# Sharing one load of the first FFN's gate and up weights between the first two row tiles

## The chip, the cores and the metric

The kernel runs on the 8 cores of one Trainium2 chip. Each core computes one of eight batch entries, so the cores do equal work and exchange nothing. The metric is device time in microseconds (us) of the slowest core.

Some executions fall into a slower state in which one die (cores 0 to 3, or 4 to 7) or both get a lower TensorE clock, whatever the kernel. The profile of the kernel before fell into the slow state on die 0; I read it on core 4, which lies on the undisturbed die, and I read core 4 of every other kernel too unless the text says otherwise. Where the cores of one run differ, I give the range or the mean of all eight (of cores 4 to 7 for the kernel before).

Engine names in the profile: PE is TensorE (matmuls), DVE is VectorE, ACT is ScalarE, POOL is GpSimd, SP issues DMA.

## The reference, cut to what matters

```python
D_MODEL, BATCH, SEQ, D_FF = 1024, 8, 4096, 2816
# x = x + 1/2 * SwiGLU_1(RMSNorm(x))
# h = RMSNorm(x);  [q,k,v | u,v_s | gates] = h @ W_in
# y_att = chunked attention (9-chunk band, relative bias);  y_sgu = spatial gating on 128-frame blocks
# x = x + (sigmoid(g_att) * (y_att @ W_att) + sigmoid(g_sgu) * (y_sgu @ W_sgu)) @ W_out
# x = x + 1/2 * SwiGLU_2(RMSNorm(x));  out = RMSNorm_final(x)
def rmsnorm(x, g):
    xf = x.astype(jnp.float32)
    y = xf * lax.rsqrt(jnp.mean(xf * xf, axis=-1, keepdims=True) + EPS)
    return (y * g.astype(jnp.float32)).astype(x.dtype)

def swiglu(h, w_gate, w_up, w_down):
    return (jax.nn.silu(h @ w_gate) * (h @ w_up)) @ w_down
```

Weights are fp32 in memory, and matmuls run in bf16. A core has 4096 rows, cut into 8 tiles of 512 rows. The factor `rsqrt(mean(x²))` is one number per row, so it can be applied before the gate and up matmuls or to their results. The change uses that.

## The kernel before: the parts that matter

Weights stream through a ring in SBUF in chunks: one gate/up chunk is 2 MB of fp32 in memory and 1 MB of bf16 in the ring. The first use of a chunk is a GpSimd DMA that casts. At one of its first uses, chosen by a rule, the bf16 chunk is also written back to a scratch in memory; from then on SP loads that half-sized copy.

```python
# pump(): as soon as the ring has room, issue the next chunk's load
if chunk not in converted:
    ...
    p.dma("pool", lambda e, dst=dst, src=src: e.dma_start(out=dst, in_=src), writes=res, sem=f"slotq{i}")
    if u >= (first_seen[chunk] * 2) % NREP:      # the rule: at which use it is written back
        converted.add(chunk); pending_wb[k] = (chunk, scr, dst, i)
else:
    p.dma("sp", ...)                             # load the bf16 copy

def dense_bank():                                # four PSUM banks in turn for all dense matmuls
    b = dn[0] % 4; dn[0] += 1; return b

def tg_buf():                                    # six work buffers in turn, for every engine
    i = tg[0] % 6; tg[0] += 1; return TG[i], ("TG", i)
```

A tile's RMSNorm is `nsq` (squares on ScalarE, summed on GpSimd or VectorE), `nstat` (a matmul with ones gives the row sums; ScalarE makes the factor), and `napply` (VectorE writes normalized bf16 to `XT`). Side work is hung on numbered pieces of the TensorE program ("hooks"). Attention of a tile is a generator that is interleaved with the next tile's FFN; at the end of each head pair it copies from PSUM, takes reciprocals on VectorE, multiplies, and lets GpSimd check the range:

```python
# attention: end of a head pair
yu, yres = tg_buf(); r2, rres = tg_buf()
... four copies PSUM -> r2, yu (VectorE and ScalarE) ...
def recip(i, j): ... e.reciprocal(out=r2[:, sl], in_=r2[:, sl])                   # VectorE, twice
def weigh(i):
    ... e.tensor_tensor(out=YA[:, hp, :], in0=yu[:], in1=r2[:], op=ALU.mult)      # VectorE
    for val, op in ((R_LO, ALU.is_ge), (R_HI, ALU.is_le)):
        buf, bres = tg_buf()
        ... gpsimd tensor_scalar(out=ok, in0=r2, ...); gpsimd tensor_tensor(OKA += ok)

# the program
load_x(0); pump()                                # x of tile 0 and all ring slots at once
for d in range(8): nsq(0, d, "dve")
nstat()
for d in range(8): napply(0, 0, d)
run_all(ffn(0, 0, False, ffn1_hooks(0)))         # FFN 1 of tile 0, whole
nxt_ffn = ffn(1, 0, True, ffn1_hooks(1))
for _ in range(4): next(nxt_ffn)
win(0, {})                                       # input projection of tile 0
for t in range(n_tiles):
    ...
    interleave(main, attention(t), n_main - 6, n_att(t))   # main: FFN 1 of tile t+1
    ...                                          # merge(t), win(t+1), FFN 2 of tile t
```

Of the kernel before, what the change touches and what calls it, by code (L numbers as in the profile page):

```python
# [17 lines left out]
T = 512  # L18
# [3 lines left out]
NREP = 3  # L22
# [21 lines left out]
class Prog:  # L44
# [58 lines left out]
    def dma(self, queue, fn, reads=(), writes=(), sem=None):  # L103
        op = _Op(queue, fn, is_dma=True, semkey=("dma", sem))
        op.idx = len(self.ops[queue])
        self._track(op, reads, writes)
        c = self.dma_counts.get(sem, 0) + 16
        self.dma_counts[sem] = c
        op.count = c
        self.ops[queue].append(op)  # L110
        return op
# [58 lines left out]
def interleave(main, side, n_main, n_side):  # L170
    done = 0
    for i in range(n_main):
        next(main, None)
        want = (i + 1) * n_side // n_main
        while done < want:
            next(side, None)
            done += 1
    for _ in side:
        pass


def build_nc(n_tiles=NT):
# [28 lines left out]
    with ExitStack() as st:  # L211
# [52 lines left out]
        EBS = X[2][:].rearrange("p a b -> p (a b)")[:, 0:8 * 384].rearrange("p (h u) -> p h u", h=8)  # L264
# [8 lines left out]
        def run(p, dry):  # L273
# [29 lines left out]
            def pump():  # L303
                while nxt[0] < len(chunk_order) and (general[0] or nxt[0] < fast_len[0]):
# [19 lines left out]
                    if chunk not in converted:  # L324
                        u = uses.get(chunk, 0)
                        uses[chunk] = u + 1
                        if chunk not in first_seen:
                            first_seen[chunk] = len(first_seen)
                        p.dma("pool", lambda e, dst=dst, src=src: e.dma_start(out=dst, in_=src),
                              writes=res, sem=f"slotq{i}")  # L330
                        if u >= (first_seen[chunk] * 2) % NREP:
# [6 lines left out]
            def get_slot(chunk):  # L338
# [7 lines left out]
                if k in pending_wb:  # L346
                    chunk_, scr, dst, i = pending_wb.pop(k)
                    p.dma("sp", lambda e: e.dma_start(out=scr, in_=dst),
                          reads=res, writes=[("SCR", chunk_)], sem=f"wb{i}")
# [7 lines left out]
            def load_x(t):  # L357
                b = t % 3
                step = 1 if t == 0 else 4
                for d in range(0, 8, step):  # L360
# [3 lines left out]
                          writes=[("X", b, i) for i in range(d, d + step)], sem=f"x{b}{d}")  # L364

            dn = [0]

            def dense_bank():
                b = dn[0] % 4
# [10 lines left out]
            def const_loads():  # L380
                p.dma("sp", lambda e: e.dma_start(out=BG[:], in_=bgate_d), writes=["BG"], sem="c2")
# [4 lines left out]
                p.dma("sp", lambda e: e.dma_start(out=EBS, in_=ebsrc_d), writes=[("X", 2, i) for i in range(8)], sem="c3")  # L386
                p.dma("pool", lambda e: e.dma_start(out=WST[:], in_=wst_d), writes=["WST"], sem="c8")
                p.dma("pool", lambda e: e.dma_start(out=IDB[:], in_=ident_d), writes=["IDB"], sem="c7")

            def const_ops():  # L390
# [13 lines left out]
                p.dma("sp", lambda e: e.dma_start(out=rt, in_=relt_d[:, 0:512]), writes=[bres], sem="c9")  # L404
# [19 lines left out]
            def bias_exp(i):  # L424
                h0 = 2 * i
                p.add("act", lambda e: e.activation(out=EB[:, h0:h0 + 2, 0:384], in_=EBS[:, h0:h0 + 2, :], func=AF.Exp),
                      reads=[("X", 2, j) for j in range(8)], writes=[("EB", i)])
# [24 lines left out]
            def nstat():  # L452
# [4 lines left out]
                p.add("act", lambda e: e.activation(out=RSTD[:], in_=bank(b), func=AF.Ln, bias=EPSB[:]),  # L457
                      reads=[rb(b), "EPSB"], writes=["RSTD"])
                p.add("act", lambda e: e.activation(out=RSTD[:], in_=RSTD[:], func=AF.Exp, scale=-0.5),  # L459
                      reads=["RSTD"], writes=["RSTD"])  # L460
# [8 lines left out]

            def store(t, d):  # L470
# [6 lines left out]
            def ffn(t, i, use_tanh, hooks=None):  # L477
                hooks = hooks or {}
                xt, xp, b3 = XT[t % 2], t % 2, t % 3
                piece = 0  # L480

                def hook():
                    nonlocal piece
                    if piece in hooks:
                        hooks[piece]()
                    piece += 1

                for f2 in (3, 8, 9, 10, 2, 0, 1, 4, 5, 6, 7):
                    Wc, wres, k = get_slot(("ffs", i, f2))
                    for a in range(2):  # L490
                        fc = 2 * f2 + a
                        W = Wc[:, a * 2048:(a + 1) * 2048]
                        bg, bu = dense_bank(), dense_bank()
                        for kc in range(8):
                            p.add("pe", lambda e, kc=kc, W=W, bg=bg: e.matmul(  # L495
                                bank(bg), lhsT=W[:, kc * 128:(kc + 1) * 128], rhs=xt[:, kc, :], start=(kc == 0), stop=(kc == 7)),
                                reads=wres + [("XT", xp, kc)], writes=[rb(bg)])
                        buf, bres = tg_buf()
                        if use_tanh:
                            p.add("act", lambda e, buf=buf, bg=bg: e.activation(out=buf[:], in_=bank(bg), func=AF.Tanh, scale=0.5),  # L500
                                  reads=[rb(bg)], writes=[bres])
                            p.add("dve", lambda e, buf=buf, bg=bg: e.scalar_tensor_tensor(  # L502
                                out=buf[:], in0=buf[:], scalar=1.0, in1=bank(bg), op0=ALU.add, op1=ALU.mult),
# [606 lines left out]
```

## Time and profile before

| | before |
|---|---|
| fast runs beside the changed kernel | 2813.39, 2810.54, 2814.45 us |
| span of core 4, granted clock | 2806.4 us, 0.994 |
| TensorE busy on core 4 | 2701.7 us, 96% |
| start of the merge of tile 0, core 4 | 335.1 us |
| from one merge to the next, tiles 1 to 6 | 342.2 (343.4 once) |
| from the merge of tile 6 to that of tile 7 | 218.1 us |

"Start of the merge" is the first matmul that reads `YA`, the attention's result.

The cores' spans and clocks of the kernel before:

```profile
core 0: 2974.2 us, clock 0.932
...
core 4: 2806.4 us, clock 0.994
```

The timeline of TensorE at the start of the kernel before (columns: start, duration, engine, line, operation, output and input tiles, shape, count; in brackets the idle time before it and what ended it):

```profile
24.05 0.77 PE L455 MATMUL ps<-ACCR,ONESR 128*128 128x512 f32 x1 [24.05 <-DVE ACCR L447]
27.33 5.22 PE L495 MATMUL ps<-XT,RING 128*128 128x512 bf16 x8 [2.52 <-DVE XT L466]
...
124.87 1.89 PE L511 MATMUL ps<-XT,RING 128*128 128x512 bf16 x7
126.60 3.62 PE L528 MATMUL ps<-HT,RING 128*128 128x512 bf16 x16
```

The first gate matmul starts at 27.3 us, and the 352 gate and up matmuls of tile 0 end at 126.6 us. At one matmul per 0.216 us they are 76.0 us of work, so 50.6 us are lost. The list of waits of TensorE (total, times, longest) shows the largest pieces:

```profile
PE ps L455 <- DVE ACCR L447: 36.0, 11, 24.0
PE ps L687 <- ACT E L691: 10.8, 7, 1.7
PE ps L495 <- DMA RING<-fsrc: 6.8, 4, 3.9
...
PE ps L701 <- DVE TG L711: 5.2, 8, 0.7
```

L455 is the row-sum matmul (24.0 us of its 36.0 at the start), L687 the attention's scores, L701 its second product. Later tiles wait 3.5 us each: they are nearly pure TensorE work.

### The profile page before, as it was taken

How to read it: one execution, taken by the hardware profiler on the slowest of the kernel's cores; microseconds unless marked ns; L12 is line 12 of the kernel's file. 1: busy time of each engine (PE TensorE's matmuls, PEld its weight loads, DVE VectorE, ACT ScalarE, POOL GpSimd, SP SyncE). 2: the span in 40 equal slices, each digit the busy share in tenths (PEclk: the TensorE clock that was granted, in tenths of full speed). 3: DMA queues.
4: the chain of work that ended last, by engine and by line, in shares of the span. 5: the costliest groups of instructions: out<-in, count | busy, mean ns of one | idle time of the engine just before them, and what ended most of it. 6: DMA issues, size and time to landing. Idle time of an engine off the chain costs nothing.

```text
span 2974.2 us, 38345 instructions; the slowest of 8 cores (2802.6 to 2974.2 us)
## 1 busy us (share of the span) xinstructions
PE 2891.8 (97%) x13034; PEld 1288.2 (43%) x13034; DVE 1248.1 (42%) x1929; ACT 893.9 (30%) x1347; POOL 503.3 (17%) x490
## 2 busy tenths in 40 slices
PE   6899999999999999999999999999999999999997
PEld 2344444444444444444444444444444444444443
DVE  2326343263432644336433464324544255455432
ACT  2323232232322323224232232323323233343221
POOL 0212312112111121111211121111211112102111
PEclk9899889998999999999999999999999999999998
DMA  9988999877777554664344443444334443433352
GB/s 194 189 166 209 176 182 176 176 208 175 176 185 184 169 144 154 176 202 170 133 142 144 161 149 135 149 144 164 139 137 140 144 148 133 141 128 123 128 182 78
DMA packets 112517, 472.41 MB, mean 159 GB/s; under 512 B 9144, under 2 KB 9144, under 8 KB 104128
## 3 DMA queue, kind: packets, MB, share of 16 engines
q1 hardware_dynamic: 90288, 371.71, 36.4%
q0 software_dynamic: 21312, 97.10, 20.6%
q8 instruction: 112, 1.84, 0.2%
q10 hardware_dynamic: 720, 1.07, 0.2%
q14 instruction: 85, 0.70, 0.1%
HBM read 501.92 MB, written 65.01 MB: 191 GB/s over the span
## 4 chain that ended last, share of the span: by engine, by line
PE 92%; DMA 3%; DVE 2%; ACT 1%; issue 1%; POOL 0%; DVEq 0%; ACTq 0%; SPq 0%; POOLq 0%
PE ps L528 22%; PE ps L511 20%; PE ps L495 20%; PE ps L810 8%; PE ps L557 6%; PE ps L820 4%; PE ps L570 3%; PE ps L839 3%; PE ps L701 2%; PE ps L687 2%; DMA ffs<-RING 1%; DMA RING<-fsrc 1%; DMA wos<-RING 0%; PE ps L644 0%; PE ps L455 0%
## 5 line engine op out<-in xcount | busy, mean ns | idle before, releaser
L495 PE MATMUL ps<-XT,RING 128*128 128x512 bf16 x2816 | 706.7, 396 | 6.8 <-DVE XT L466 2.5
L511 PE MATMUL ps<-XT,RING 128*128 128x512 bf16 x2816 | 706.8, 397 | 6.3 <-DVE HT L515 6.3
L528 PE MATMUL ps<-HT,RING 128*128 128x512 bf16 x2816 | 660.7, 399 | 0.0
L528 PEld LDWEIGHTS ps<-HT,RING 128*128 128x128 bf16 x2816 | 285.2, 102 | 362.7 <-issue 145.2
L515 DVE TENSOR_TENSOR HT<-ps,TG 128x512 bf16<-128x512 f32 x352 | 241.1, 685 | 466.8 <-PE ps L511 419.0
L511 PEld LDWEIGHTS ps<-XT,RING 128*128 128x128 bf16 x2816 | 281.4, 101 | 351.3 <-issue 121.2
L495 PEld LDWEIGHTS ps<-XT,RING 128*128 128x128 bf16 x2816 | 281.8, 101 | 350.5 <-issue 119.6
L444 POOL TENSOR_TENSOR ACC<-ACC,TG 128x512 f32<-128x512 f32 x186 | 239.8, 1289 | 1075.4 <-ACT TG L441 1074.3
L441 ACT ACTIVATE TG<-X 128x512 f32<-128x512 f32 x224 | 140.2, 627 | 547.5 <-DVE X L534 453.4
L534 DVE SCALAR_TENSOR_TENSOR X<-ps,X 128x512 f32<-128x512 f32 x128 | 88.4, 692 | 424.7 <-PE ps L528 420.8
L810 PE MATMUL ps<-XT,RING 128*128 128x512 bf16 x1024 | 261.1, 401 | 0.0
L506 ACT ACTIVATE TG<-ps 128x512 f32<-128x512 f32 x176 | 105.0, 597 | 449.0 <-PE ps L495 435.4
L691 ACT ACTIVATE E<-ps 128x1024 bf16<-128x1024 f32 (+1 forms) x240 | 168.4, 702 | 197.3 <-PE ps L687 174.3
L732 POOL TENSOR_SCALAR TG<-TG 128x512 bf16<-128x512 f32 x64 | 98.8, 1543 | 587.3 <-DVE TG L721 577.6
L502 DVE SCALAR_TENSOR_TENSOR TG<-TG,ps 128x512 f32<-128x512 f32 x176 | 119.7, 680 | 168.5 <-ACT TG L500 145.3
L500 ACT ACTIVATE TG<-ps 128x512 f32<-128x512 f32 x176 | 105.1, 597 | 266.6 <-PE ps L495 236.1
L557 PE MATMUL ps<-XT,RING 128*128 128x512 bf16 x768 | 178.2, 395 | 0.0
L694 DVE TENSOR_TENSOR E<-E,EB 128x1024 bf16<-128x1024 bf16 (+1 forms) x240 | 127.5, 531 | 94.9 <-ACT E L691 93.9
L824 DVE SCALAR_TENSOR_TENSOR TG<-TG,ps 128x512 f32<-128x512 f32 x128 | 87.8, 687 | 182.1 <-PE ps L820 155.3
L810 PEld LDWEIGHTS ps<-XT,RING 128*128 128x128 bf16 x1024 | 103.8, 102 | 135.1 <-issue 60.2
L815 ACT ACTIVATE TG<-ps,BG 128x512 f32<-128x512 f32 x128 | 87.5, 687 | 241.1 <-PE ps L810 241.0
L466 DVE SCALAR_TENSOR_TENSOR XT<-X,G,RSTD 128x512 bf16<-128x512 f32 x192 | 135.6, 746 | 30.9 <-ACT RSTD L459 30.9
(91 smaller groups left out, 1937.5 us busy)
## 6 DMA issues: line engine op xcount, KB each, us to landing
RING<-ffs SPq DMA_DIRECT2D x131, 1024.0 KB, 5.0
RING<-wds SPq DMA_DIRECT2D x97, 704.0 KB, 4.4
RING<-fsrc POOLq DMA_DIRECT2D x45, 1024.0 KB, 13.4
RING<-mgs SPq DMA_DIRECT2D x48, 768.0 KB, 4.3
RING<-wis SPq DMA_DIRECT2D x29, 1024.0 KB, 4.8
ffs<-RING SPq DMA_DIRECT2D x22, 1024.0 KB, 12.2
RING<-wd POOLq DMA_DIRECT2D x31, 704.0 KB, 11.2
out<-X SPq DMA_DIRECT2D x32, 512.0 KB, 4.1
```

The lines of the kernel that those rows point to most:

```text
L441: p.add("act", lambda e: e.activation(out=buf[:], in_=src, func=AF.Square, scale=1.0 / 32.0), reads=[xres], writes=[bres])
L444: p.add(eng, lambda e: e.tensor_tensor(out=ACC[:], in0=ACC[:], in1=buf[:], op=ALU.add), reads=["ACC", bres], writes=["ACC"])
L466: p.add("dve", lambda e: e.scalar_tensor_tensor(out=dst, in0=src, scalar=G4[:, which * 8 + d:which * 8 + d + 1], in1=RSTD[:], op0=ALU.mult ...
L495: p.add("pe", lambda e, kc=kc, W=W, bg=bg: e.matmul(bank(bg), lhsT=W[:, kc * 128:(kc + 1) * 128], rhs=xt[:, kc, :], start=(kc == 0), stop= ...
L502: p.add("dve", lambda e, buf=buf, bg=bg: e.scalar_tensor_tensor(out=buf[:], in0=buf[:], scalar=1.0, in1=bank(bg), op0=ALU.add, op1=ALU.mul ...
L511: p.add("pe", lambda e, kc=kc, W=W, bu=bu: e.matmul(bank(bu), lhsT=W[:, 1024 + kc * 128:1024 + (kc + 1) * 128], rhs=xt[:, kc, :], start=(k ...
L515: p.add("dve", lambda e, buf=buf, bu=bu, fc=fc: e.tensor_tensor(out=HT[:, fc, :], in0=bank(bu), in1=buf[:], op=ALU.mult), reads=[rb(bu), b ...
L528: p.add("pe", lambda e, fc=fc, W=W, by=by: e.matmul(bank(by), lhsT=W[:, fc * 128:(fc + 1) * 128], rhs=HT[:, fc, :], start=(fc == 0), stop= ...
L557: p.add("pe", lambda e, kc=kc, W=W, b=b, cc=cc: e.matmul(bank(b), lhsT=W[:, kc * 512 + cc * 128:kc * 512 + (cc + 1) * 128], rhs=XT[t % 2][ ...
L691: p.add("act", lambda e: e.activation(out=ee, in_=PS[2][:].rearrange("p (h c) -> p h c", h=2)[:, :, 0:n], func=AF.Exp), reads=[rb(4), rb(5 ...
L694: p.add("dve", lambda e: e.tensor_tensor(out=ee, in0=ee, in1=EB[:, 2 * hp:2 * hp + 2, u0:u0 + n], op=ALU.mult), reads=[("E", i % 2), ("EB" ...
L810: p.add("pe", lambda e, kc=kc, W=W, bgt=bgt, j=j: e.matmul(bank(bgt), lhsT=W[:, j * 1024 + kc * 128:j * 1024 + (kc + 1) * 128], rhs=XT[t % ...
```

## The change

The intent is to lose less at the start. Only x of tile 0 and one chunk (in four parts) load first. TensorE begins on x that is converted but not normalized ("raw"), and tile 0's row factor is applied where results leave PSUM. The gate/up chunks then serve tiles 0 and 1 together, tile 1 four chunks behind, so each fp32 chunk feeds twice the matmuls. Transfers not needed yet are "paced": they wait for the newest TensorE instruction in program order. The down projections and the attention follow:

- before: gate/up/down(0), input projection(0), then gate/up/down(1) interleaved with attention(0), 56 pieces of the FFN;
- after: gate/up(0 and 1), down(0), last chunk of (1), input projection(0), then down(1), 16 pieces, interleaved with attention(0).

The core of the diff:

```diff
+        if paced:
+            op.deps.append(self.ops["pe"][-1])        # a DMA waits for PE's newest instruction
 ...
-                        if u >= (first_seen[chunk] * 2) % NREP:
+                        if k == 0:                    # first chunk in four parts
+                            for j in range(4): ...
+                        else:                         # the second waits for the last part of x of tile 0
+                            ... reads=[("X", 0, 7)] if k == 1 else () ...
+                        if u >= (0 if first_seen[chunk] < 19 else first_seen[chunk] % 2 + 1):
 ...
+            n_dense = [4]                             # 6 banks during the joint stage
 ...
+            def gu_chunk(t, f2, slot, mode, hook, ht=ht_own, free=True):
+                banks = [dense_bank() for _ in range(4)]        # four banks at once (before: two)
+                ...                                             # modes tanh, silu, and for tile 0:
+                        VectorE: buf = bank(bg) * RS0           # raw: row factor on the gate result
+                        ScalarE: buf = Silu(buf)
+                        VectorE: buf = buf * RS0                # and for the up result
+                if mode == "raw_first":                         # first chunk, follows x piece by piece
+                    for kc in range(8):
+                        nraw(t, 0, kc)
+                        for j in range(4): mm(j, kc)
+                        ...
+            def gate_up_both(hooks):
+                LAG = 5
+                for n in range(len(F2) + LAG - 1):
+                    if n >= LAG:
+                        f2 = F2[n - LAG + 1]
+                        writeback(slots[f2])
+                        yield from gu_chunk(1, f2, slots[f2], "silu", hook, ht_second)
+                    if n < len(F2):
+                        f2 = F2[n]
+                        slots[f2] = get_slot(("ffs", 0, f2), wb=(n == 0))
+                        n_dense[0] = 6
+                        yield from gu_chunk(0, f2, slots[f2], "raw" if n else "raw_first", hook, free=(n == 0))
 ...
+                add_hook(hk, 4, P(load_x, 1))                   # x of tile 1, paced
 ...
-            run_all(ffn(0, 0, False, ffn1_hooks(0)))
-            nxt_ffn = ffn(1, 0, True, ffn1_hooks(1))
+            run_all(gate_up_both(both_hooks()))
+            run_all(down(0, 0, 0.5, Hooks(hk)))
+            run_all(gu_chunk(1, F2[0], get_slot(("ffs", 0, F2[0])), "silu", Hooks(hk), ht_second))
             win(0, {})
 ...
+                    if t == 0:
+                        main = down(1, 0, 0.5, Hooks(hk), ht_second)
+                        interleave(main, attention(t), 14, n_att(t))
+                    else:                                       # attention starts 6 pieces later than before
+                        main = ffn(t + 1, 0, True, ffn1_hooks(t + 1))
+                        interleave(main, attention(t), N_FFN - 6, n_att(t), 6)
```

## The prediction

> **What bounds it now.** The fast runs take 2810.5 and 2813.4 us; the profile fell in the slow state, so I read core 4 of the fast die (2806.4 us, clock 0.994). TensorE is the limit: its busy row is 9 in 38 of 40 slices, matmuls start every 0.216 us, and the chain of waits is 89% TensorE. Only the start is loose. By the timeline the first gate matmul starts at 27.3 us, and the gate/up of tile 0 (352 matmuls, 76 us of pure work) ends at 126.6: 50.6 us lost. The wait list gives 24.0 us for the first sum of squares (x lands late because five weight chunks were issued with it; DMA busy share 1.0), 2.5 for the scaling, the rest gaps of 1.9 to 4 us for fp32 chunks, squares that wait for x of tile 1, four exponential-table switches (1.28 us each), and constant memsets (3.5 us). The merge of tile 0 starts at 333.3.
>
> **What the change does.**
> - Start: only x and chunk 0 load first. By the DMA queue table of the first 60 us a chunk costs about 6.3 us of all 16 engines and x about 6.8 (estimates), so both have landed near 17 us. The x conversion is a tensor_scalar on fp32 in SBUF; the Trainium skill (VectorE: DVE Perf Modes, mode 2x_2P) says such an op runs at twice the rate; here a like one took 546 ns against 745. Chunk 0 needs all four parts before matmul 4, and its first matmuls are cold (0.43 us apart in the trace at 32 us, as TensorE: Matmul & The Clock Gate, Part 1, says). Chunk 0 then ends near 23 us, against 38.7.
> - Chunks 1 to 4 serve tile 0 alone: one per 6.9 us of TensorE, while DMA also moves x of tile 1 and one write-back. I expect waits here; chunk 4 ends near 61 us, about 26 us behind pure work.
> - From then on one chunk serves 13.8 us, against about 10 us of DMA with its write-back: no DMA waits until the down projection, where 19 early write-backs may cost 0 to 5 us.
> - Added VectorE work: two 0.69 us multiplies in each of 22 gate tiles, off the critical path.
> - Attention of tile 0 now spreads over 14 down pieces, not 50 pieces. Pairs of steps in one piece make the scores wait for the exponential (0.6 to 1.0 us) and VectorE (reciprocals of 1.75 us) is dense: 4 to 10 us given back.
> - Later tiles: attention starts six pieces later. Today every ffn1 starts with a 1.67 us wait of the scores for an exponential stuck behind a table load, and a 0.65 us one later. Six tiles: 6 to 12 us saved.
> - Fewer fp32 reloads: DMA is not waited for there, so nothing.
>
> **Sum.** Merge of tile 0 at about 317 instead of 333 (-16), later tiles -10 to -12. Predicted 2785 us, range 2768 to 2799; faster by over 2% 0.06, within 2% 0.92, slower 0.02.
>
> **What would show it.** First matmul near 14 us and chunk 0 done near 23; DMA waits on fsrc only in the first 65 us; joint gate/up (21 of 22 chunks) ending near 173 us, down of tile 0 near 212; waits scores<-exponential bunched in the down of tile 1; the 1.67 us waits gone in tiles 2 to 6; total TensorE wait down from 75 us on core 4 to about 50.
>
> **What would make it wrong.** Better: chunk 0 and x land by 12 us and chunks 1 to 4 keep pace: then 2770. Worse: write-backs and fp32 loads of the down weights and input projection queue up (they are now close together), or attention in the short down stage stalls on VectorE: then the start's gain is given back, 2800 or more.

## The result, and the profile after

All ratios here are the mean time of one kernel's fast runs over that of the other's in the same rounds, and the times that I quote are of fast runs.

The changed kernel's fast runs took 2841.0 and 2842.5 us (two further runs were slow), beside 2813.39, 2810.54 and 2814.45 us before. The ratio is 1.0103, with a 95% interval of 1.0074 to 1.0132. The change made the kernel 1.0% slower. The prediction was 2785 us, 1.0% faster, with a range of 2768 to 2799. On core 4 the span grew from 2806.4 to 2834.3 us:

```profile
core 4: 2834.3 us, clock 0.991
...
die 1 (median of its cores): 2836.0 us, clock 0.991
```

The start on TensorE now, from the timeline of core 4:

```profile
13.42 0.58 PE L537 MATMUL ps<-XT,RING 128*128 128x512 bf16 x1 [13.42 <-DMA RING<-fsrc]
...
19.52 8.92 PE L537 MATMUL ps<-XT,RING 128*128 128x512 bf16 x29 [0.74 <-DMA RING<-fsrc]
...
49.12 1.01 PE L537 MATMUL ps<-XT,RING 128*128 128x512 bf16 x2 [3.20 <-DVE HT L561]
...
57.75 1.89 PE L537 MATMUL ps<-XT,RING 128*128 128x512 bf16 x8 [0.20 <-DMA RING<-fsrc]
71.29 0.76 PE L478 MATMUL ps<-ACCR,ONESR 128*128 128x512 f32 x1 [11.65 <-DVE ACCR L470]
...
82.55 1.91 PE L537 MATMUL ps<-XT,RING 128*128 128x512 bf16 x3 [2.74 <-DVE XT L489]
85.13 10.17 PE L537 MATMUL ps<-XT,RING 128*128 128x512 bf16 x35 [0.67 <-DVE XT L489]
...
196.58 3.62 PE L596 MATMUL ps<-HT,RING 128*128 128x512 bf16 x16
```

TensorE does start at 13.4 us, as predicted. But it loses time until 85 us. The largest wait after the first, 11.65 us, is for the row sum of tile 1 (L478), because x of tile 1 landed late: its two halves at 56.4 and 66.7 us. The row sum stands in TensorE's program behind the first eight matmuls of chunk 4, the last chunk that tile 0 has to itself (the line at 57.75), so the rest of that chunk waits with it. This is when ScalarE could begin to square the two halves:

```profile
56.43 0.63 ACT L460 ACTIVATE ACC<-X 128x512 f32<-128x512 f32 x1 [2.55 <-DMA X<-xT]
66.79 2.19 ACT L464 ACTIVATE TG<-X 128x512 f32<-128x512 f32 x4 [5.03 <-DMA X<-xT]
```

The joint stage covers 21 of the 22 chunk uses, 672 matmuls or 145.2 us of pure work, and ends at 196.6 us: 51.4 us are lost, where one tile had lost 50.6 before. The start has gained nothing. By the list of waits up to there, 21.1 us of the 51.4 are for fp32 chunks (13.4 of them the first wait of all), 11.7 for the row sum, 3.4 for the scaling of tile 1 and 3.2 for VectorE's work on tile 0. The rest, some 12 us, is no wait: matmuls that follow each other more slowly than 0.216 us, about half of it between 71 and 90 us, and the two row sums themselves.

The waits of the whole kernel after:

```profile
PE ps L795 <- DVE TG L805: 21.4, 18, 6.8
PE ps L478 <- DVE ACCR L470: 21.1, 11, 11.7
PE ps L537 <- DMA RING<-fsrc: 21.1, 7, 13.4
PE ps L781 <- ACT E L785: 6.9, 6, 1.4
PE ps L738 <- ACT TG L550: 5.4, 6, 0.9
```

L478 is the old L455, L781 the old L687, L795 the old L701; L738 is the spatial gating's mixing matmul, which did not wait before. In the lists the row sums fell by 15 us, the chunks rose by 14.3 and the attention's second product by 16.2. The first two are partly one thing under two names: the first wait of the kernel, 24.0 us for a row sum before, is now 13.4 us for a chunk.

Where L795 waits longest is in the short stage that runs down(1) with attention(0). The timeline there:

```profile
313.29 1.49 POOL L826 TENSOR_SCALAR TG<-TG 128x512 bf16<-128x512 f32 x1
314.88 0.59 ACT L807 ACTIVATE TG<-ps 64x512 f32<-64x512 f32 x1 [6.89 <-POOL TG L826]
314.89 0.69 DVE L803 COPY TG<-ps 64x512 f32<-64x512 f32 x1 [3.33 <-POOL TG L826]
...
316.44 1.01 PE L795 MATMUL ps<-E,VR 128*128 128x512 bf16 x2 [6.77 <-DVE TG L805]
```

The wait list names VectorE for the 6.77 us, but VectorE itself stood still for 3.33 us of them: the copies out of PSUM needed work buffers that GpSimd's range check of the previous head pair (L826) still read.

The milestones on core 4 (each column from the start or from the milestone before, in us):

| | merge of tile 0 | tile 1 | tile 2 | tiles 3 to 6 | tile 7 | TensorE's last matmul |
|---|---|---|---|---|---|---|
| before | 335.1 | 342.2 | 343.4 | 342.2 each | 218.1 | 182.8 |
| after | 353.4 | 344.4 | 344.8 | 342.0 each | 224.7 | 182.5 |

The span ends 16 us after the last matmul in both. So +18.3 us by the merge of tile 0, and +9.6 after it, of which +6.6 in the last tile (5.0 on five other cores).

Of the 18.3 us, the joint stage accounts for 0.8 (51.4 us lost against 50.6). The other 17.5 were lost between its end and the merge: TensorE's waits there sum to 19.6 us, before to 4.9 (from 126.6 us to the merge), and 16.0 of the 19.6 lie in the stage of down(1) with attention(0).

In tile 2, core 4 is the mildest case. Over the eight cores that tile took 344.8 to 350.3 us after, mean 347.9; before, on cores 4 to 7, 342.2 to 343.8, mean 342.9. The cores with the longest spans, 1 and 5, had 350.3. So for the whole chip tile 2 costs about 5 us, and not the 1.4 of core 4.

### The profile page after: what moved, and what is told of

It is laid out like the page before. It is cut to its first block, busy times and chain, and to the rows that moved or that the text cites. A ratio compares the mean times of both kernels' runs of the same rounds, so it can differ in the third digit from the quotient of the medians.

```text
span 2839.4 us, 38314 instructions; the slowest of 8 cores (2832.8 to 2839.4 us)
## 1 busy us (share of the span) xinstructions
PE 2724.4 (96%) x13034; PEld 1246.3 (44%) x13034; DVE 1272.6 (45%) x1975; ACT 897.0 (32%) x1348; POOL 473.0 (17%) x467
## 2 busy tenths in 40 slices
DMA packets 110532, 461.90 MB, mean 163 GB/s; under 512 B 9080, under 2 KB 9080, under 8 KB 102272
## 4 chain that ended last, share of the span: by engine, by line
PE 88%; DMA 6%; DVE 3%; issue 2%; ACT 1%; POOL 1%; DVEq 0%; ACTq 0%; SPq 0%; POOLq 0%
PE ps L537 38%; PE ps L596 20%; PE ps L904 8%; PE ps L651 6%; PE ps L914 4%; PE ps L933 4%; PE ps L664 3%; DMA RING<-fsrc 2%; PE ps L795 2%; PE ps L781 2%; DMA X<-xT 2%; DMA RING<-wd 1%; DMA ffs<-RING 1%; POOL TG L826 0%; DVE TG L803 0%
## 5 line engine op out<-in xcount | busy, mean ns | idle before, releaser
L537 PE MATMUL ps<-XT,RING 128*128 128x512 bf16 x5632 | 1272.1, 381 | 33.1 <-DMA RING<-fsrc 29.0
L537 PEld LDWEIGHTS ps<-XT,RING 128*128 128x128 bf16 x5632 | 547.3, 98 | 678.7 <-issue 59.0
L596 PE MATMUL ps<-HT,RING 128*128 128x512 bf16 x2656 | 583.1, 379 | 1.7 <-DMA RING<-wd 1.6
L561 DVE TENSOR_TENSOR HT<-ps,TG 128x512 bf16<-128x512 f32 x332 | 228.0, 687 | 374.8 <-PE ps L537 328.6
L596 PEld LDWEIGHTS ps<-HT,RING 128*128 128x128 bf16 x2656 | 258.5, 98 | 311.4 <-issue 4.9
L467 POOL TENSOR_TENSOR ACC<-ACC,TG 128x512 f32<-128x512 f32 x162 | 208.8, 1289 | 880.3 <-ACT TG L464 879.9
L904 PE MATMUL ps<-XT,RING 128*128 128x512 bf16 x1024 | 242.0, 379 | 0.0
L550 ACT ACTIVATE TG<-ps 128x512 f32<-128x512 f32 x176 | 105.1, 597 | 428.0 <-PE ps L537 413.8
L826 POOL TENSOR_SCALAR TG<-TG 128x512 bf16<-128x512 f32 x64 | 99.5, 1554 | 637.3 <-DVE TG L815 636.2
L651 PE MATMUL ps<-XT,RING 128*128 128x512 bf16 x768 | 168.4, 379 | 0.0
L546 DVE SCALAR_TENSOR_TENSOR TG<-TG,ps 128x512 f32<-128x512 f32 x154 | 103.6, 673 | 130.8 <-ACT TG L544 109.4
L918 DVE SCALAR_TENSOR_TENSOR TG<-TG,ps 128x512 f32<-128x512 f32 x128 | 87.1, 685 | 154.3 <-PE ps L914 129.9
L904 PEld LDWEIGHTS ps<-XT,RING 128*128 128x128 bf16 x1024 | 99.6, 98 | 120.8 <-issue 3.2
L544 ACT ACTIVATE TG<-ps 128x512 f32<-128x512 f32 x154 | 92.0, 597 | 188.4 <-PE ps L537 180.1
L489 DVE SCALAR_TENSOR_TENSOR XT<-X,G,RSTD 128x512 bf16<-128x512 f32 x184 | 130.0, 745 | 28.4 <-ACT RSTD L482 28.4
L795 PE MATMUL ps<-E,VR 128*128 128x512 bf16 (+1 forms) x480 | 104.7, 300 | 21.8 <-DVE TG L805 21.3
L664 PE MATMUL ps<-RING,XT 128*128 128x512 bf16 x512 | 115.1, 379 | 1.7 <-DVE XT L489 1.7
## 6 DMA issues: line engine op xcount, KB each, us to landing
RING<-fsrc POOLq DMA_DIRECT2D x37, 1024.0 KB, 16.2
```

The costliest lines, as they stand in the source:

```text
L467: p.add(eng, lambda e: e.tensor_tensor(out=ACC[:], in0=ACC[:], in1=buf[:], op=ALU.add), reads=["ACC", bres], writes=["ACC"])
L489: p.add("dve", lambda e: e.scalar_tensor_tensor(out=dst, in0=src, scalar=G4[:, which * 8 + d:which * 8 + d + 1], in1=RSTD[:], op0=ALU.mult ...
L537: p.add("pe", lambda e: e.matmul(bank(b), lhsT=Wc[:, j * 1024 + kc * 128:j * 1024 + (kc + 1) * 128], rhs=xt[:, kc, :], start=(kc == 0), st ...
L561: p.add("dve", lambda e: e.tensor_tensor(out=dst, in0=bank(bu), in1=buf[:], op=ALU.mult), reads=[rb(bu), bres], writes=[dres])
L596: p.add("pe", lambda e, fc=fc, W=W, by=by, hap=hap: e.matmul(bank(by), lhsT=W[:, fc * 128:(fc + 1) * 128], rhs=hap, start=(fc == 0), stop= ...
L651: p.add("pe", lambda e, kc=kc, W=W, b=b, cc=cc: e.matmul(bank(b), lhsT=W[:, kc * 512 + cc * 128:kc * 512 + (cc + 1) * 128], rhs=XT[t % 2][ ...
```

## The experiments

Each edit is relative to the changed kernel unless it says otherwise. All results were correct against the reference except that of x1_memset. Ratios are to the kernel before.

### Why does x of tile 1 land late: x1_unpaced and wb_paced

Theory A: pacing issues it too late. Theory B: it is issued into DMA engines that are already full.

```diff
-                add_hook(hk, 4, P(load_x, 1))
+                add_hook(hk, 4, P(load_x, 1, False))          # x1_unpaced: same place, not paced
```

> The changed kernel, but the load of x of tile 1 no longer waits for TensorE, so it is issued near 20 us instead of 31.7. Theory A (the early gain is eaten because x of tile 1 lands too late, at 67 us, and the squares and the row sum that wait for it stand in line before tile 0's work on ScalarE and TensorE): if its late issue is the reason, it lands about 10 us earlier, the 11.7 us wait for the sum of squares shrinks by about as much and the joint gate/up ends near 186 us instead of 196.6. Rival B (the DMA engines are simply full until then, whoever goes first): x lands earlier but chunks 1 to 4 land later by the same, the waits move to the weights and the gate/up still ends within 3 us of 196.6. Rival C (the added VectorE chain of tile 0 holds the banks): no change at all beyond 3 us.

Measured: three fast runs of 2841.5 to 2843.0 us, ratio 1.0091 (1.0062 to 1.0121): nothing gained. x of tile 1 was issued at 19.24 us instead of 31.68, and TensorE still waited:

```profile
68.47 0.76 PE L478 MATMUL ps<-ACCR,ONESR 128*128 128x512 f32 x1 [7.38 <-DVE ACCR L470]
...
82.05 8.31 PE L537 MATMUL ps<-XT,RING 128*128 128x512 bf16 x29 [0.68 <-DVE XT L489]
```

Issuing it 12.4 us earlier moved the row sum by 2.8 us, and the smooth part by 3.1. It was also paid for at once: the wait for the second chunk grew from 1.04 to 6.18 us. On the mean of the eight cores the joint stage ends 1.4 us sooner. Pacing is not the cause.

```diff
-                          reads=res, writes=[("SCR", chunk_)], sem=f"wb{i}")
+                          reads=res, writes=[("SCR", chunk_)], sem=f"wb{i}", paced=paced)
-                        writeback(slots[f2])
+                        writeback(slots[f2], True)            # wb_paced: write-backs wait for TensorE
```

> The changed kernel, but the write-backs of chunks 1 and later wait until TensorE has come to their second use. In the trace of the changed kernel write-backs 1 and 2 are issued at 33 and 39 us, beside x of tile 1 and the chunks that are still missing. Theory A2 (these write-backs, 2 of about 3.4 us of all engines each, delay x of tile 1): x lands about 7 us earlier, near 60 us, and the joint gate/up ends near 188 us. Rival C (the VectorE chain of tile 0 sets the pace) or a limit in the load of x itself: gate/up end within 2 us of 196.6. The rest of the kernel is the same in both theories.

Measured: four fast runs of 2846.7 to 2852.5 us, ratio 1.0115 (1.0093 to 1.0138). Two of the three write-backs left the window, and x of tile 1 still landed in two halves by 56.2 and 65.3 us. (That the whole became slower still comes later: the input projection's first chunk, behind the postponed write-backs, is waited for at 247.7 us, for 4.60 us.) This run allows an account of DMA between 18.7 and 65.3 us, from the queue table of that window (queue, kind, packets, MB, share of 16 engines):

```profile
q0 software_dynamic: 1360, 5.24, 71.5%
q1 hardware_dynamic: 1328, 3.15, 24.6%
```

The window is 46.6 us long. The first line is the five fp32 chunks issued there: 0.715 · 46.6 / 5 = 6.7 us of all 16 engines each. The second is 2 MB of x and one write-back of 1 MB, 11.5 us together. The sum fills 96% of the window. So theory B holds: when x of tile 1 is issued, four fp32 chunks are still in flight (the last of them prefetched, not needed until later), and all of them share the engines. The Trainium skill (Trainium Kernel Development and Optimization, Key Constraints) says just this of transfers from the SP, ACT and POOL queues, that they run on the same 16 engines and interleave. The trace agrees: x, with nothing else left in its own queue, took 27.6 us in the median from issue to landing.

### How much is that one late transfer worth: x1_memset and lag3

x1_memset takes the transfer away: GpSimd fills x of tile 1 with zeros instead. The result is wrong (relative error 0.50).

```diff
-                add_hook(hk, 4, P(load_x, 1))
+            for h in range(2):
+                p.add("pool", lambda e, h=h: e.memset(X[1][...half h...], 0.0), writes=[...])
```

> Wrong result on purpose. The changed kernel, but x of tile 1 is filled with zeros by GpSimd instead of loaded, so it is there near 30 us and takes nothing from the DMA engines. It measures what that one transfer costs. Theory A' (x of tile 1 is the last of what tile 1 has to wait for: it shares the DMA engines with five fp32 chunks that tile 0 needs first, and 7.7 us per chunk is more than I reckoned): the 11.7 us wait and the slow clock after it vanish, what is left is one chunk per about 8 us, and the joint gate/up ends near 172 us instead of 196.6. Rival C (the VectorE chain of tile 0 with its two extra multiplies): gate/up still ends later than 188 us.

Measured: four fast runs of 2836.1 to 2841.4 us, ratio 1.0078 (1.0061 to 1.0095). On core 4 the wait for the row sum is gone (on the others it is 0.5 to 3.8 us), and the smooth part starts at 74.2 us instead of 85.1; on core 4 the row sum of tile 0's second norm, just after down(0), comes at 226.4 us instead of 237.7. But of these 11 us only about 8 reach the end of core 4 (2826.4 us) and about 4 the time of the slowest core: tile 2 took 348.3 us instead of 344.8. On the mean of the eight cores the joint stage ends 8.0 us sooner and the span is 6.2 us shorter.

lag3 does it correctly: x of tile 1 is issued as soon as x of tile 0 has landed, ahead of the first write-back, and tile 1 runs two chunks behind tile 0, not four.

```diff
-                LAG = 5
+                LAG = 3                                       # and tile 1's norm hooks 8 pieces earlier
-                add_hook(hk, 4, P(load_x, 1))
+            load_x(1, False, [("X", 0, 7)])                   # before gate_up_both
```

> The changed kernel with two things moved: tile 1 follows tile 0 by two chunks instead of four, and its x is issued right after x of tile 0, together with chunk 1. Then only three chunks and both x have to be in before tile 1 begins, and each later chunk serves 13.8 us of matmuls. Theory A' (the limit is the DMA work that must come before tile 1 may start): x of tile 1 lands by about 38 us, gate/up ends near 174 us instead of 196.6, and the whole is 18 to 24 us faster. Rival C, or a limit per transfer that does not depend on what is in flight: gain under 8 us.

Measured: fast runs of 2838.4, 2842.4 and 2866.9 us, ratio 1.0136 (1.0085 to 1.0187, a wide interval). x of tile 1 landed at 23.4 and 39.3 us on core 4. There the start became much better, and tile 2 much worse:

```profile
47.99 0.47 PE L478 MATMUL ps<-ACCR,ONESR 128*128 128x512 f32 x1 [2.45 <-DVE ACCR L470]
...
60.86 29.39 PE L537 MATMUL ps<-XT,RING 128*128 128x512 bf16 x126 [0.67 <-DVE XT L489]
...
848.50 8.84 PE L537 MATMUL ps<-XT,RING 128*128 128x512 bf16 x39 [1.86 <-DMA RING<-fsrc]
...
890.68 4.91 PE L596 MATMUL ps<-HT,RING 128*128 128x512 bf16 x22 [1.93 <-DMA RING<-wd]
```

The merge of tile 0 started at 344.9 us instead of 353.4, and the interval of tile 2 rose from 344.8 to 352.0, with waits for weight chunks between 830 and 900 us. So on core 4 the late x costs about 9 us up to the merge of tile 0, and most of that gain is given back in tile 2.

The other cores don't all follow. The joint stage ends at 187.2 to 198.5 us (mean 193.0) in lag3, at 195.0 to 199.1 (mean 197.5) in the changed kernel and at 185.3 to 192.2 (mean 189.5) in x1_memset. On cores 2, 5 and 7 of lag3 the row sum waits for nothing, but the second chunk, now behind x, is waited for instead (10.3 to 13.8 us), and the stage ends at 194.8 to 198.5. So the transfer of x is worth 8.0 us on the mean of the cores, and sending it first saves 4.5 of them: it changes the order, not the sum of what DMA has to move.

### Is the raw start worth anything: no_raw

```diff
-                        yield from gu_chunk(0, f2, slots[f2], "raw" if n else "raw_first", hook, free=(n == 0))
+                        yield from gu_chunk(0, f2, slots[f2], "silu", hook, free=(n == 0))
+            for d in range(8): nsq(0, d, "dve")
+            nstat()
+            for d in range(8): napply(0, 0, d)                # tile 0 normalized before gate_up_both
```

> The changed kernel without the raw start: tile 0 is normalized first, as before the change, and its gates leave PSUM in one step; the joint use of the chunks stays. If the raw start is worth something by itself, gate/up ends later than 196.6 us by the 4 to 6 us that the first matmuls wait for the factor and its eight multiplies. If x of tile 1 sets the end of the early stage (theory A'), it ends within 2 us of 196.6, for the extra time fits into that wait. If the VectorE chain of the raw tile is a cost (rival C), it ends earlier, by 3 us or more.

Measured: three fast runs near 2841 us (2840.1 to 2841.9), ratio 1.0088 (1.0071 to 1.0104), the same as the changed kernel's; three more runs were slow. Its profile fell into the slow state on die 1, so this is core 0, on the undisturbed die:

```profile
20.16 0.77 PE L478 MATMUL ps<-ACCR,ONESR 128*128 128x512 f32 x1 [20.16 <-DVE ACCR L470]
23.45 34.12 PE L537 MATMUL ps<-XT,RING 128*128 128x512 bf16 x136 [2.52 <-DVE XT L489]
70.57 0.77 PE L478 MATMUL ps<-ACCR,ONESR 128*128 128x512 f32 x1 [13.00 <-DVE ACCR L470]
...
81.68 8.58 PE L537 MATMUL ps<-XT,RING 128*128 128x512 bf16 x39 [0.28 <-DVE XT L489]
```

TensorE starts 10 us later than in the changed kernel and is smooth 3 to 4 us earlier (81.7 against 85.6 on the same core, 85.1 on core 4). In between it runs through four chunks of tile 0 without a wait for one. The raw start had only moved the wait from in front of the first matmul to between the chunks; x of tile 1 is waited for in both. But it was not free either: without it the joint stage ends at 190.6 to 194.1 us on cores 0 to 3 (mean 192.1), and in the changed kernel at 195.0 to 199.1 there (mean 197.5). That is the third case of the expectation, a cost of the raw mode. No run separates its VectorE chain from the rest of it. The gain is not seen in the total because tile 2 took 351.5 us on the mean of these cores instead of 347.5.

### The short attention stage: okbufs

Theory: the 6.77 us wait is a shortage of buffers. While tile 0's attention runs, `XT[1]` is free, so its eight pieces can hold the row sums and the results of the range check.

```diff
-                    r2, rres = tg_buf()
+                    q = 2 * (items[i][0] % 2)                 # t == 0 only
+                    r2 = XT[1][:, q:q + 2, :].rearrange("p a b -> p (a b)").bitcast(F32)
-                        buf, bres = tg_buf()
+                            q = 4 + 2 * (hp % 2) + n_ok       # t == 0 only
+                            ok, bres = XT[1][:, q, :], ("XT", 1, q)
```

> The changed kernel, but in the attention of tile 0 the row sums, their reciprocals and GpSimd's range check use buffers of their own (the input of tile 1's gate/up, free by then) instead of the six that rotate among all. Theory D (the waits of 6.8 and 4.0 us for the copies out of PSUM are a lack of buffers: GpSimd, 1.5 us per check, still reads them): both waits fall under 1 us, the down projection of tile 1 takes about 58 us instead of 70.8, and the whole is 11 to 13 us faster. Rival E (VectorE is too dense in this stage, 44 us of 70): the same waits stay under another name and the stage stays over 66 us.

Measured: three fast runs of 2832.4 to 2833.7 us, ratio 1.0060 (1.0031 to 1.0090). The stage, from its first matmul to the first of the merge, took 62.1 us instead of 70.7, and on the mean of the eight cores the merge of tile 0 came 8.7 us sooner. The longest wait in it is now

```profile
313.24 0.59 PE L795 MATMUL ps<-E,VR 128*128 128x512 bf16 x2 [3.48 <-DVE TG L811]
```

and ends with VectorE's own copies, queued behind reciprocals of 1.75 us. The buffers were half of the wait. What is left fits a dense VectorE, which was busy for 44.0 of 70 us in this stage of the changed kernel; no run tests that alone.

### The later tiles: banks

Theory: `gu_chunk` takes four PSUM banks at once where the kernel before took two, so a mixing matmul that comes between them gets a bank whose gate result ScalarE has just begun to read. The edit takes two at a time.

```diff
-                banks = [dense_bank() for _ in range(4)]
+                banks = []                                    # raw_first still takes four
 ...
                 for a in range(2):
+                    if mode != "raw_first":
+                        banks += [dense_bank(), dense_bank()]
```

> The changed kernel, but the PSUM banks of a gate/up chunk are taken two at a time, when they are used, as before the change, not four at once. Theory F (a bank that the sgu mixing takes in the middle of a chunk is the one that the gate matmuls have just filled, so TensorE waits for its reader): the wait of the mixing for ScalarE, 0.89 us once in each of six tiles, and 1.86 us in the last one, are gone; the last tile, 6.7 us longer than before the change, loses 4 to 7 us, the others 0.9 each: 9 to 12 us faster in all. Rival G (the later place of the mixing and of attention in the stage is the cause): no change beyond 2 us, the waits stay.

Measured: four fast runs of 2833.9 to 2836.7 us, ratio 1.0070 (1.0047 to 1.0093). All waits of L738 for ScalarE are gone, tiles 3 to 6 take 341.0 us instead of 342.0, and tile 7 takes 221.1 instead of 224.7. The wait that went, in the changed kernel's tile 1:

```profile
462.48 0.41 PE L738 MATMUL ps<-WST,HT 128*64 128x128 bf16 x8 [0.89 <-ACT TG L550]
```

### Together, and where the backlog comes from: lag3_fix, fix_conv

lag3_fix is lag3, okbufs and banks in one kernel.

> The three mended parts together: tile 1 two chunks behind with its x early, buffers of its own for the range check of tile 0's attention, banks taken in pairs. If the three causes are separate, their gains add up: 22 + 8.5 + 6 us less than 2842, about 2805 us, which is 0.3 to 0.5% faster than the kernel before the change. If part of the gain of one is given back in another stage, the sum is smaller and the kernel before stays ahead (over 2814).

Measured: three fast runs of 2821.8 to 2822.6 us, ratio 1.0021 (1.0001 to 1.0041). The sum of the three gains, 2805 us, was not reached. The merge of tile 0 started between 336.5 and 347.4 us on the eight cores and tile 1 took 341.5, but tile 2 took 346.2 to 351.3. Next, what fills DMA in tile 2. These are windows of 50 us on core 4, with the columns: window, its length, busy time and count for PE, PEld, DVE, ACT and POOL, granted clock, DMA share, GB/s. First the kernel before:

```profile
700.00:750.00 50.00, 47.44 (x216) 21.36 (x219) 17.63 (x27) 18.39 (x27) 10.20 (x10) 1.00 0.72 202
...
850.00:900.00 50.00, 48.12 (x224) 21.98 (x226) 18.46 (x29) 13.71 (x19) 8.75 (x7) 1.00 0.79 221
```

and the changed kernel:

```profile
700.00:750.00 50.00, 49.45 (x226) 22.40 (x230) 24.84 (x37) 17.61 (x25) 7.72 (x9) 1.00 1.02 201
...
850.00:900.00 50.00, 47.76 (x218) 21.48 (x221) 13.28 (x20) 10.65 (x15) 10.12 (x11) 1.00 1.02 200
```

The changed kernel moves 461.90 MB in all, before 472.41 MB, yet it fills DMA here, where the kernel before leaves a tenth to a quarter free (its shares over the four windows from 700 to 900 us are 0.72, 0.84, 0.88 and 0.79). From 700 to 900 us it issues 25 fp32 loads of weights and only 3 loads of bf16 copies; before it was 15 and 15. fix_conv tests the new conversion rule as the cause: it puts the old rule back for all chunks but the first 19.

```diff
-                        if u >= (0 if first_seen[chunk] < 19 else first_seen[chunk] % 2 + 1):
+                        if u >= (0 if first_seen[chunk] < 19 else (first_seen[chunk] * 2) % NREP):
```

> lag3_fix with one thing undone: which use of a late weight chunk is written back as bf16 follows the rule of before the change (first, third, second use in turn) instead of second and third use in turn. Theory H (the new rule puts fp32 loads and write-backs together in tile 2, where the DMA share is 1.0 from 750 to 900 us, and time that the early stage wins is waited away there): the time from the merge of tile 1 to that of tile 2, 342 to 344 us before the change, 345 to 350 after it and 346 to 351 in lag3_fix, comes back to at most 344 on all cores, and the whole is 4 to 7 us faster than lag3_fix, about 2817. If that interval is long for another reason (attention starts later in the stage), it stays over 346.

Measured: three fast runs of 2819.5 to 2820.9 us, ratio 1.0011 (0.9982 to 1.0040). Tile 2 fell to between 341.0 and 344.0 us on all cores, so the rule was the cause of the crowding there. But tile 1 rose to 346.7 to 351.8 on five cores, with waits for fp32 chunks of other weights. Most of the cost had moved forward by one tile: on the mean tile 2 fell by 6.6 us and tile 1 rose by 4.5. With interval ends this close, this run does not separate fix_conv from lag3_fix in total time.

### Spreading the rest: lag4_ok and lag4_defer

lag4_ok: tile 1 three chunks behind tile 0, x of tile 1 early, okbufs, banks, the old rule, and the mixing matmuls of the last FFN at their old pieces.

> fix_conv with tile 1 three chunks behind instead of two, so that TensorE has tile 0's fourth chunk to do while x of tile 1 is normalized (in lag3 it stood from 54 to 61 us for that), and the mixing of the second FFN back at its old place. Theory A' says the early stage is set by what must have landed plus the 18 us from x to the scaled input: the smooth part starts with 33 to 36 us lost instead of 39.5; the old place of the mixing gives 2 to 4 us in the last tile (221 to 218 us between the last two merges). About 2808 to 2812 us, 0.1 to 0.3% faster than the kernel before.

Measured: four fast runs of 2814.9 to 2822.4 us, ratio 1.0008 (0.9985 to 1.0030). The last tile is back at 218.1 us and tiles 3 to 6 at 341.0 to 341.3; the spans of the cores run from 2798.5 to 2816.2 us, and the slowest decides.

lag4_defer gives attention(0) more TensorE work to hide behind, in place of okbufs: three gate/up chunks of tile 1 are kept back and run with it, with tanh in place of silu, so that ScalarE needs no table switch between them and the exponentials.

```diff
+                        def rest():
+                            for f2 in F2[len(F2) - 3:]:
+                                yield from gu_chunk(1, f2, get_slot(("ffs", 0, f2)), "tanh_half", hook, ht_second)
+                            yield from down(1, 0, 0.5, hook, ht_second)
-                        interleave(main, attention(t), 14, n_att(t))
+                        interleave(main, attention(t), 25, n_att(t))
```

> As lag4_ok, but instead of buffers for the range check, three of tile 1's gate/up chunks are left out of the joint stage and run with attention of tile 0, at the cost of loading these three chunks again as bf16. Then attention has 26 pieces of dense work beside it instead of 14. Theory D/E (in the short stage VectorE and the buffers cannot keep up with the rate at which attention is asked for): the waits for copies out of PSUM fall under 1 us each, attention of tile 0 and the work beside it lose 3 us or less instead of 12, and the total is 4 to 8 us below lag4_ok, 2802 to 2807. If the stage is limited by the chain scores, exponential, product itself and not by its rate, it loses as much as in lag4_ok.

Measured: two fast runs, 2816.4 and 2817.9 us; the other two were slow, and no ratio is given. The attention stage keeps three waits over 0.4 us, of 0.82, 0.64 and 2.85 us, on core 4. A new one stands at the end of the joint stage:

```profile
177.99 2.72 PE L605 MATMUL ps<-HT,RING 128*128 128x512 bf16 x6 [9.21 <-DVE HT L568]
```

Here down(0) waits for tile 0's last hidden values, which in raw mode pass VectorE twice more; with three chunks kept back no work of tile 1 hides that.

### Without the raw mode: noraw_defer

lag4_defer with the edit of no_raw. (In the text, "four pieces behind" is the setting LAG = 4, which means three chunks.)

> The kernel of lag4_defer (x of tile 1 issued early, the second tile four pieces behind the first, banks taken in pairs, old conversion rule, three gate/up chunks of tile 1 kept for attention(0)), but tile 0 normalized first and run through plain Silu, so without the two extra VectorE multiplies per gate tile. The raw mode was worth nothing in no_raw, and in lag4_defer it left a 9.2 us wait of down(0) for VectorE at the end of the joint stage and a 10 us wait for chunk 1. Theory R (the raw mode now only costs): gates of tile 0 start near 24 us, the wait for chunk 1 shrinks below 4 us, the 9.2 us wait goes, merge of tile 0 starts at 328 to 338 on the cores, interval of tile 1 341 to 343, fast runs 2800 to 2810, ratio to before 0.996 to 0.999. Rival S (the slowest core is set by the DMA backlog of tiles 1 and 2, which moves but does not go away): merge 0 earlier on most cores, but one or two cores have an interval of 348 or more in tile 1 or 2, and the fast runs stay at 2813 to 2820, ratio 1.000 to 1.002.

Measured: five fast runs of 2806.2 to 2810.2 us, beside before at 2813.9 to 2816.6; ratio 0.9975, interval 0.9961 to 0.9989. It beats both kernels, by 0.25% over the kernel before. The longest waits of core 4, and then TensorE's timeline of core 0 at the end of the joint stage:

```profile
PE ps L478 <- DVE ACCR L470: 30.4, 10, 21.8
PE ps L805 <- DVE TG L815: 13.0, 16, 2.9
PE ps L539 <- DMA RING<-fsrc: 9.3, 3, 3.7
```

```profile
173.49 3.40 PE L605 MATMUL ps<-HT,RING 128*128 128x512 bf16 x15
181.53 2.72 PE L605 MATMUL ps<-HT,RING 128*128 128x512 bf16 x6 [4.64 <-DVE HT L568]
```

The 9.2 us wait is halved (4.64 us on core 4 too), not gone as I had expected; the first row sum again waits 21 us, and the total is still the best. On core 4 the merge of tile 0 starts at 335.3 us, where the kernel before has 335.1. The six intervals after it sum to 2047.1 us, before 2054.4. So all of its gain on core 4, 7.3 us, comes from the later tiles: the attention that starts later, with the banks taken in pairs as before the change. The joint start itself ends even there (over the eight cores 328.1 to 341.3 us). The raw mode, however, is what this kernel leaves out of lag4_defer, and lag4_defer's two fast runs lay level with the kernel before (2815.2 to 2817.5 us in their rounds). Each set against the kernel before in its own rounds, the two differ by 7 to 8 us; with two fast runs on one side that is an estimate of what the raw mode costs here.

## Why the prediction was wrong, point by point

The prediction put the merge of tile 0 at about 317 us, counted from 333.3 before, which is the first matmul of the merge and not the first that reads `YA`. Counted so it came at 351.7 on core 4. That is 35 us of the error of 56 (2841 less 2785). The remaining 21 lie in the later tiles.

1. **"Chunk 0 then ends near 23 us"**: it ended at 28.4. The last part of chunk 0 came at 19.5 us and not 17, and the 29 matmuls behind it took 8.9 us, 0.31 us each, and not 6.3. I had allowed for a few cold matmuls, citing the Trainium skill (TensorE: Matmul & The Clock Gate, Part 1, which puts a cold matmul of 512 columns at 426.7 ns and a warm one at 215.7). The trace has 6 of these matmuls in each of the windows 20 to 22 and 22 to 24 us, and 9 in the next, but its granted clock reads 1.00 there; so it shows the slow pace and not its cause. (In the records of single instructions they start 0.43 us apart until 24.6 us and 0.22 us apart after it, as the page has it.) Later, from 60 to 90 us, the clock itself reads 0.66.
2. **"Chunk 4 ends near 61 us, about 26 us behind pure work"**: this is the step that failed. The joint stage was never smooth before 85 us, and ended at 196.6 us instead of 173: 23.6 us of the error. The waits for chunks were priced about right. From the end of chunk 0 to the eighth matmul of chunk 4 (28.4 to 59.6 us) TensorE lost 8.7 us against pure work over three and a quarter chunks, and I had allowed 10.4 for four; a chunk cost 6.7 us of all DMA engines against my 6.3. What the path left out is the row sum of tile 1, which stands in TensorE's program in the middle of chunk 4: there TensorE waited 11.65 us for x of tile 1, and chunk 4 ended near 79 us. I had named the transfer ("DMA also moves x of tile 1 and one write-back"), but I had not added up what it shares the engines with, a prefetched fifth chunk among it, and so not asked when it lands: 66.7 us. x1_unpaced and wb_paced show that pacing and write-backs are not the cause; x1_memset shows that the transfer is worth 11 us there on core 4 and 8.0 on the mean. That the fifth chunk delays it is argued from the queue table; no run leaves it out. The rest is the first chunk (5.4 us late), the raw mode, the scaling of tile 1 (3.4 us) and matmuls at a slow pace after the wait; I did not measure each alone.
3. **Raw start "so both have landed near 17 us"**: the first matmul came near 14 us, as expected (13.4), and it gained nothing. no_raw starts 10 us later, is smooth earlier and ends the joint stage about 5 us sooner on the mean of its undisturbed die. The scaling itself was priced right: 0.483 us per raw conversion against 0.745 for the scaled one, a ratio of 0.65 and not quite the half that the Trainium skill (VectorE: DVE Perf Modes, Mode 2×_2P) lets one expect.
4. **"Off the critical path"** (the two extra VectorE multiplies per gate tile): not quite. A wait of 3.2 us ends with the chain that they are part of in the changed kernel, and one of 9.2 us in lag4_defer, which falls to 4.6 without them.
5. **Attention of tile 0, "4 to 10 us given back"**: right mechanism, wrong size. The waits over 0.4 us between 284 and 354 us sum to 16.0 us, and the merge waits 2.25 more for `YA`. I foresaw the pairs of scores steps (4.7 us) and the dense VectorE. I did not foresee GpSimd holding the buffers: okbufs got 8.6 us of the stage back.
6. **Later tiles, "6 to 12 us saved"**: the 1.67 us waits for the exponential did vanish in the middle tiles, as predicted. In their place came 0.89 us for a bank (banks removes it) and a second wait of 0.66 us in the attention, so a tile went from 342.2 to 342.0 us. In the last tile the moved mixing matmuls met the bank order (6.6 us on core 4; banks returns 3.6; lag4_ok, with the hooks moved back as well, all). Of this point, 1.2 us per tile can be had: noraw_defer has 341.0.
7. **"Fewer fp32 reloads: DMA is not waited for there, so nothing"**: wrong. Fewer bytes in total, but the new rule crowds fp32 reloads and write-backs into tile 2. The changed kernel loses 1.4 us there on core 4 and about 5 on the mean of the cores. Kernels that started sooner lost more (means of 348.9 us in x1_memset and 349.3 in lag3, against 347.9), until fix_conv moved the crowd. On core 4 of lag3 most of the earlier start went there; on the mean of its cores 1.5 of 3.7 us did.
8. **"Total TensorE wait down from 75 us to about 50"**: it rose to about 95. The three largest entries alone sum to 63.6 us after.

Of the prediction's list of what would make it wrong, "attention in the short down stage stalls on VectorE" came true, and fp32 loads did queue up, though one tile later than I had said. What stays open: how much of the joint stage's 51.4 us each of its waits would give back if it went alone (removing x gave 8.0 on the mean), and why the cores of one run differ by 10 us in tile 1 or 2 with equal programs.

## What to carry to other kernels

At the start of a kernel that waits for DMA, add up the engine time of everything that will be in flight before the last thing needed lands, prefetches included; starting TensorE sooner on part of the data only moves the wait. Issue first what gates the next dependent step, here x of the second tile, but expect only what the order can give: on three of eight cores the wait merely moved to the chunk behind it. Read every core: core 4 lost 1.4 us in tile 2, and core 5, one of the two that set the time, 8.1. And when work is moved into a shorter stage, look for each engine that holds a shared buffer or bank there: a wait names only the engine that ended it, not the one that had held that engine up.

## What the Trainium skill lacked or had wrong

- **ScalarE: Activation LUTs** (Terms) puts a table load at about 2.7 us. The same page, under "What ACT_TABLE_LOAD costs", splits this into 1283 ns for the load and about 1380 ns of drain. In the kernel before, the 31 loads at the norm's line and all other loads on core 4 took 1.283 us each, so the first part agrees. The second does not show: in the changed kernel the load at 72.49 us begins 0.02 us after the activation before it ends (72.47), and the next activation starts when it ends (73.78). Costing a switch at 2.7 us would have doubled it.
- **GPSIMD Engine Reference** (4.1 Engine selection) says that operations with one input run at roughly line rate there. The range check, one input of 128x512 fp32 to bf16, took 1.555 us on GpSimd (64 of them on core 4 after; the profile's spans on this engine are rough), where a VectorE operation of the same shape and types took 0.546 us. That check is what held the buffers.
- **DMA: Bandwidth & Descriptors** (Anatomy of one DMA) gives a fit of 2.0 us plus bytes over 436 GB/s. For a chunk of 2 MB in and 1 MB out this is 4.4 us by the bytes written and 6.8 by the bytes read, an estimate from that page. The page does not say which counts in a cast. In wb_paced a chunk took 6.7 us of all engines; that is a share of the engines' time and not the time of one transfer, so it does not decide between the two. What the page has no figure for is the landing time under load: 28 us in the median for five such chunks with x between them.
